# Another written order for the attention steps of a hybrid mixer

## The chip, the cores and the metric

The kernel runs on one core of a Trainium2 chip. The metric is device time in microseconds (us) of one execution. The core's engines work beside one another, each through its own queue in order: PE (TensorE, the matmuls), DVE (VectorE), ACT (ScalarE), POOL (GpSimd) and SP (SyncE, which issues the DMAs).

## The reference

Two layers, each on 256 tokens of width 1024 in float32. A layer adds half of a gated feed-forward (width 2816), then a mixer, then half of a second feed-forward:

```python
for l in range(DEPTH):
    x = x + 0.5 * swiglu_ffn(x, ffn1...)
    h = rms_norm(x, mix_norm[l])
    (fq, fk, fv, ff, gu, gv, nq, nkc, nvc, nks, nvs, nkw, nvw, ng, pz) = split(h @ w_in[l])
    o_a = fox_mixer(fq, fk, fv, ff)         # 4 heads, softmax attention with a forget bias
    o_b = gmlp_mixer(gu, gv)                # 4 gated groups
    o_c = nsa_mixer(nq, nkc, ..., ng)       # 4 heads: compressed + selected + window attention
    o_d = pool_mixer(pz)                    # 4 groups of running means
    x = x + concat([o_a, o_b, o_c, o_d]) @ w_out[l]
    x = x + 0.5 * swiglu_ffn(x, ffn2...)
```

With 256 tokens the selected and the window branch of nsa_mixer both are plain causal softmax attention over all tokens, over one key head of width 64 that four query heads share; the compressed branch has 15 keys that come out of a small two-layer network over windows of 32 tokens.

## The kernel before, in words

Everything is kept transposed, 128 features on the partitions and 256 tokens along the row. Weights and activations of the large products are split in two parts of reduced precision: a part h (ACT copies the raw weights, L122) and the remainder lo (DVE subtracts h from them, L123); a product is two or three matmuls (mm2, L147; mm3, L141). A weight block of 128 x 2048 thus costs a DMA into one of four raw buffers, two copies on ACT and two subtractions on DVE, the first halves ahead of the second. Where split() is called (by the first step of a generator such as out_part or z_proj), those four instructions stand in the ACT and DVE queues at that place.

The mixer first makes the projections. From the place named `here` on, its order is written out by hand as a list of calls, and pin() (L102) adds an edge from each PE, DVE and ACT instruction to the next of the same engine, so each of the three queues keeps exactly the order of the list. DMA issues (SP), POOL's instructions, and instructions outside the list, such as the next feed-forward's first weight copies, are placed between by the framework's scheduler.

In the list there are six attention jobs, each a pair of heads: F0 and F1 (fox) and N0 to N3 (nsa: two pairs, and for each the selected and the window branch). A job has these steps:

- scores(jb), L765: four matmuls into two PSUM banks; then on DVE four reductions that add the mask and take the row maxima (L779), and on ACT four exponentials with their sums (L781).
- scale(jb), L784: DVE's reciprocal of the sums (L787), a gate (L789) and four multiplications of the probabilities (L792).
- trans(jb), L794: six PE transposes into two banks (L799) and two copies out by ACT (L801).
- values(jb), L804: eight matmuls (L811) that need those copies.
- done(jb), L814: for an nsa pair one more matmul with the compressed branch's weights (L817); then the result is split into h (ACT, L134) and remainder (DVE, L135).

Between these stand filler blocks of PE work that need nothing from the attention: zq (a projection), cmp_hidden (the first layer of the compression network), pool_mix and pool_out (whose split is L137 on ACT and L138 on DVE), and steps of the output product, out_part (L829). The latter has four generators: w00 and w01 for the first half of the output columns, w10 and w11 for the second, the last digit for the half of the inputs. The first `go` of one calls split(); each of the 16 following steps is one mm3. The compressed branch goes through cmp_gelu (three pieces, parted by yields), cmp_out (two pieces; the first has DVE's vbd copies, L502), cmp_keys, cmp_scores (three pieces: mask; maximum and exponential, L738 to L740; sums and weights, L743 to L748) and cmp_weights (PE transposes, L755), which needs the last piece of cmp_scores and is needed by done(N1) and done(N3).

PSUM has eight banks, all drawn from one pool; a bank is taken at the first write and given back behind the last reader.

Of the kernel before, what the change touches and what calls it, by code (L numbers as in the profile page):

```python
# [70 lines left out]
def tile_macaron(ctx, tc, xT, g0, const0, consts, params, w13, w2, wA, wB, wD, wC, wE, wcmp, wo, out):  # L71
# [15 lines left out]
    def bank_a():  # L87
        a = banks.tile([128, 512], F32, name="a", tag="bank")
        return a

    def bank_h():
        h = banks.tile([128, 512], F32, name="h", tag="bank")
        return h
# [5 lines left out]
    def halves(s):  # L99
        return s.rearrange("p (a n) -> p a n", a=2)  # L100
# [248 lines left out]
    def mixer(l, norm, par):  # L349
        def Pm(name, p=128):  # L350
            o, w = _PAR[name]
            return par[0:p, o:o + w]
# [49 lines left out]
        def head_norm(ps, ht, nh, width):  # L402
            nt = [s2(), s2()]
            for t in range(2):
                nc.vector.tensor_tensor(nt[t][:, :width].rearrange("p (h d) -> p h d", d=64),
                                        ps[t][:, :width].rearrange("p (h d) -> p h d", d=64),
                                        ht[:, t, :nh].unsqueeze(2).to_broadcast([128, nh, 64]), op=ALU.mult)
            return nt
# [113 lines left out]
        def cmp_keys():  # L522
            p = bank_h()
            nc.tensor.transpose(p[:, 0:NC], e.kcn[0:NC, :], ident[0:NC, 0:NC])
            for par2 in range(2):
                rows = slice(64 * par2, 64 * par2 + 64)
                nc.vector.tensor_copy(kcz[rows, par2, 0:NC], p[rows, 0:NC])
# [81 lines left out]
        def pool_out():  # L609
            pw = Pm("pw").rearrange("p (c e) -> p c e", c=2)  # L610
            py = halves(bank_h())
            for c in range(2):
                nc.tensor.matmul(py[:, c, :], pw[:, c, :], e.po[:, c, :], start=True, stop=True)
            for c in range(2):
                oT[6 + c] = split_scaled(py[:, c, :], Pm("pscale")[:, c:c + 1])
# [9 lines left out]
        def b_post():  # L625
            nt = head_norm(e.pB, e.hB, 6, 384)
            nqk = w1p.tile([128, 2, 448], F32)
            nq = nqk[:, :, 0:384].rearrange("p t (h d) -> p t h d", d=64)
            for t in range(2):
                nc.vector.tensor_tensor(nqk[:, t, 0:384], nt[t][:, 0:384], Pm("ngain"), op=ALU.mult)  # L630
            ra = w1p.tile([128, 2, 6, 16], F32)
            rc = w1p.tile([128, 2, 6, 16], F32)

            def tab(i, c0, c1):
                return rope[:, i, :, c0:c1].unsqueeze(2).to_broadcast([128, 2, 6, c1 - c0])

            nc.vector.tensor_tensor(ra, nq[:, :, :, 0:16], tab(0, 0, 16), op=ALU.mult)
            nc.vector.tensor_tensor(rc[:, :, :, 0:8], nq[:, :, :, 8:16], tab(1, 0, 8), op=ALU.mult)
            nc.vector.tensor_tensor(rc[:, :, :, 8:16], nq[:, :, :, 0:8], tab(1, 8, 16), op=ALU.mult)
            nc.vector.tensor_tensor(nq[:, :, :, 0:16], ra, rc, op=ALU.add)  # L640
            nc.vector.tensor_copy(nqk[:, :, 384:448], nqk[:, :, 256:320])
            e.nqk = nqk

        def b_heads():
            nqT, nkT = halves(s2()), halves(s2())
            p = transposed([e.nqk[:, t, 128 * i:128 * i + 128] for i in range(2) for t in range(2)])
            nc.scalar.activation(nqT, p, AF.Copy)

            p = transposed([e.nqk[:, t, 256 + 64 * i:384 + 64 * i] for i in range(2) for t in range(2)])
            nc.scalar.activation(nkT, p, AF.Copy)  # L650
            e.nqT, e.nkT = nqT, nkT
# [111 lines left out]
        tcols = (slice(0, 128), slice(128, 384))  # L763

        def scores(jb):  # L765

            q, ks = jb.qk()
            s = [bank_h(), bank_h()]
            for t, c in enumerate(tcols):
                for i, rows in enumerate(half_rows):  # L770
                    nc.tensor.matmul(s[i][:, c], q[rows, 128 * t:128 * t + 128], ks[i][rows, 0:128 * t + 128],
                                     start=True, stop=True)
            bias = e.bias[jb.pair] if jb.branch is None else [(mask[:, 128:256], mask)] * 2
            jb.s = [s2(), s2()]
            jb.sm = at.tile([128, 2, 2], F32, name="sm")
            nm = at.tile([128, 2, 2], F32, name="nm")
            for i in range(2):
                for t, c in enumerate(tcols):
                    nc.vector.tensor_tensor_reduce(out=jb.s[i][:, c], in0=s[i][:, c], in1=bias[i][t], op0=ALU.add,  # L779
                                                   op1=ALU.min, scale=-1.0, scalar=3e38, accum_out=nm[:, t, i:i + 1])  # L780
                    nc.scalar.activation(jb.s[i][:, c], jb.s[i][:, c], AF.Exp, scale=-1.0, bias=nm[:, t, i:i + 1],  # L781
                                         accum_out=jb.sm[:, t, i:i + 1])

        def scale(jb):  # L784

            rv = at.tile([128, 2, 2], F32, name="rv")
            nc.vector.reciprocal(rv, jb.sm)  # L787
            if jb.branch is not None:
                nc.vector.tensor_tensor(rv, rv, e.g4[:, :, 2 * jb.pair:2 * jb.pair + 2, jb.branch], op=ALU.mult)  # L789
            for i in range(2):  # L790
                for t, c in enumerate(tcols):
                    nc.vector.tensor_scalar(jb.s[i][:, c], jb.s[i][:, c], rv[:, t, i:i + 1], None, op0=ALU.mult)  # L792

        def trans(jb):  # L794
            jb.pT = []
            for i in range(2):
                p = bank_h()
                for n in range(3):
                    nc.tensor.transpose(p[:, 128 * n:128 * n + 128], jb.s[i][:, 128 * n:128 * n + 128], ident)  # L799
                pT = s2()  # L800
                nc.scalar.activation(pT[:, 0:384], p[:, 0:384], AF.Copy)  # L801
                jb.pT.append(pT)

        def values(jb):  # L804

            if jb.branch != 2:
                e.acc[jb.pair] = bank_a()
            acc = e.acc[jb.pair]
            for tj, c, o in ((0, slice(0, 256), 0), (1, slice(256, 384), 128)):
                for i, rows in enumerate(half_rows):  # L810
                    nc.tensor.matmul(acc[rows, o:256], e.v[tj][:, jb.v[i]:jb.v[i] + 64], jb.pT[i][:, c],  # L811
                                     start=jb.branch != 2 and tj == 0, stop=jb.branch is None and tj == 1)

        def done(jb):  # L814
            acc = e.acc[jb.pair]
            if jb.branch is not None:
                nc.tensor.matmul(acc[:, 0:256], vbd[:, jb.pair, :], e.pcT, start=False, stop=True)  # L817
            oT[jb.pair + (0 if jb.branch is None else 4)] = split_scaled(acc[:, 0:256], None)
# [21 lines left out]
        N0, N1, N2, N3, F0, F1 = jobs  # L840
# [13 lines left out]
        def go(gen, n=1):  # L854
            for _ in range(n):
                next(gen, None)
# [15 lines left out]
        w00, w01 = out_part(0, 0, wacc), out_part(0, 1, wacc)  # L872
# [2 lines left out]
        cmp_hidden(0, 1)  # L875
        b_stats()
        scores(F0)
        go(zq)
        fox_bias(1)
        cmp_hidden(1, 0)  # L880
        scale(F0)
        b_post()
        scores(F1)
        go(zq)
        trans(F0)
        b_heads()
        cmp_hidden(1, 1)
        pool_mix()
        scale(F1)
        values(F0)  # L890
        scores(N0)
        gelu = cmp_gelu()
        go(gelu)
        trans(F1)
        go(w00, 4)
        done(F0)
        go(gelu)
        scale(N0)
        pool_out()
        values(F1)  # L900
        scores(N1)
        go(w01)
        done(F1)
        go(w00, 4)
        go(gelu)
        trans(N0)
        scale(N1)
        go(w00, 4)
        values(N0)
        scores(N2)  # L910
        go(w00, 5)
        outs = cmp_out()
        go(outs)
        trans(N1)
        wacc1 = [halves(bank_a()), halves(bank_a())]
        w10, w11 = out_part(1, 0, wacc1), out_part(1, 1, wacc1)
        go(w10)
        go(w01, 4)
        go(outs)
        values(N1)  # L920
        scale(N2)
        scores(N3)
        go(w01, 4)
        trans(N2)
        cmp_keys()
        go(w10, 3)
        cs = cmp_scores()
        go(cs)
        scale(N3)
        go(w11)  # L930
        go(w10, 1)
        values(N2)
        go(cs)
        go(w10, 4)
        trans(N3)
        go(w10, 5)
        go(cs)
        values(N3)
        go(w10, 4)
        cmp_weights()  # L940
        go(w11, 4)
        done(N1)
# [135 lines left out]
```

## Time and profile before

| | before |
|---|---|
| median of 3 runs | 983.79 us (981.37 to 986.28) |
| the profiled execution, its own time | 982.34 us |
| its span, first to last instruction | 980.5 us |
| mean granted TensorE clock | 0.996 |
| busy: PE / weight loads / DVE / ACT | 98% / 85% / 71% / 54% |
| instructions | 14915 |

The span is what the timeline covers; the execution's own time has some 1.8 us around it. Busy time of PE is that of its matmuls, which overlap one another: a matmul's duration is longer than the step to the next, so the pace of a block is read as the difference between the start of a block and the start of the next. [...] The first mixer's written list runs from about 232 to 300 us, the second's from about 715 to 784 us; times below are of the first unless said otherwise.

### The profile page before, as it was taken

How to read it: one execution, taken by the hardware profiler on the slowest of the kernel's cores; microseconds unless marked ns; L12 is line 12 of the kernel's file. 1: busy time of each engine (PE TensorE's matmuls, PEld its weight loads, DVE VectorE, ACT ScalarE, POOL GpSimd, SP SyncE). 2: the span in 40 equal slices, each digit the busy share in tenths (PEclk: the TensorE clock that was granted, in tenths of full speed). 3: DMA queues.
4: the chain of work that ended last, by engine and by line, in shares of the span. 5: the costliest groups of instructions: out<-in, count | busy, mean ns of one | idle time of the engine just before them, and what ended most of it. 6: DMA issues, size and time to landing. Idle time of an engine off the chain costs nothing. (4 is left out here: it accounts for less than half of the span.)

```text
span 980.5 us, 14915 instructions
## 1 busy us (share of the span) xinstructions
PE 964.3 (98%) x5840; PEld 838.0 (85%) x5840; DVE 698.6 (71%) x1256; ACT 530.6 (54%) x971; POOL 66.0 (7%) x67
## 2 busy tenths in 40 slices
PE   8999999999989999999999999999998999999998
PEld 6888888898869888888888888889987898888887
DVE  5987776575778777776667777755666787777751
ACT  7655555363566555655445655544545665555530
POOL 2000000031102000000010000001220030000000
PEclk9999999999999999999999999999999999999999
DMA  8965554445426655555555555545453455555530
GB/s 306 338 230 196 172 191 174 159 145 215 173 94 233 232 173 189 197 172 196 191 172 187 200 172 188 197 152 184 169 203 114 150 211 175 177 196 188 177 108 17
DMA packets 28150, 179.28 MB, mean 183 GB/s; under 512 B 3248, under 2 KB 5168, under 8 KB 8240
## 3 DMA queue, kind: packets, MB, share of 16 engines
q1 hardware_dynamic: 27792, 178.19, 52.1%
q8 instruction: 46, 0.75, 0.3%
q10 hardware_dynamic: 288, 0.14, 0.1%
q14 instruction: 24, 0.20, 0.1%
HBM read 177.27 MB, written 1.05 MB: 182 GB/s over the span
## 5 line engine op out<-in xcount | busy, mean ns | idle before, releaser
L123 DVE TENSOR_TENSOR lo<-r,h 128x1024 fp32r<-128x1024 f32 (+4 forms) x346 | 391.7, 1148 | 163.4 <-ACT h L122 162.7
L149 PE MATMUL h<-hl,h 128*128 128x512 f32 x1408 | 498.7, 399 | 1.4 <-ACT h L122 0.8
L122 ACT ACTIVATE h<-r 128x1024 fp32r<-128x1024 f32 (+4 forms) x346 | 327.8, 973 | 268.1 <-issue 230.6
L150 PE MATMUL h<-hl,lo 128*128 128x256 f32 x1408 | 395.3, 281 | 0.5 <-DVE lo L123 0.5
L149 PEld LDWEIGHTS h<-hl,h 128*128 128x128 f32 x1408 | 264.4, 188 | 67.9 <-DVE hl L138 1.5
L150 PEld LDWEIGHTS h<-hl,lo 128*128 128x128 f32 x1408 | 265.8, 189 | 2.1 <-DVE lo L123 2.1
L149 PE MATMUL a<-hl,h 128*128 128x512 f32 x704 | 246.9, 395 | 0.0
L150 PE MATMUL a<-hl,lo 128*128 128x256 f32 x704 | 197.3, 280 | 0.0
L149 PEld LDWEIGHTS a<-hl,h 128*128 128x128 f32 x704 | 131.9, 187 | 31.5 <-DVE hl L135 0.9
L150 PEld LDWEIGHTS a<-hl,lo 128*128 128x128 f32 x704 | 133.0, 189 | 0.0
L234 DVE SCALAR_TENSOR_TENSOR x<-a,x 128x256 f32<-128x256 f32 x80 | 32.9, 421 | 49.0 <-PE a L150 45.3
L304 DVE TENSOR_TENSOR s<-h,s 128x256 f32<-128x256 f32 x176 | 65.9, 415 | 1.1 <-ACT s L303 1.1
L305 DVE TENSOR_TENSOR s<-s,rb 128x512 f32<-128x512 f32 x88 | 60.9, 692 | 2.8
L134 ACT ACTIVATE hl<-s 128x256 fp32r<-128x256 f32 x92 | 38.2, 417 | 43.4 <-DVE s L308 33.9
L303 ACT ACTIVATE s<-h 128x256 f32<-128x256 f32 x176 | 56.5, 371 | 2.7 <-PE h L150 2.7
L211 POOL TENSOR_TENSOR s<-s 128x512 f32<-128x512 f32 x12 | 16.8, 1402 | 593.3 <-ACT s L207 593.3
L143 PE MATMUL a<-h,hl 128*128 128x384 f32 (+2 forms) x128 | 45.8, 358 | 0.0
L307 ACT ACTIVATE s<-s 128x256 f32<-128x256 f32 x88 | 35.5, 404 | 17.9 <-DVE s L305 17.8
L145 PE MATMUL a<-h,hl 128*128 128x384 f32 (+2 forms) x128 | 45.0, 351 | 0.0
L144 PE MATMUL a<-lo,hl 128*128 128x384 f32 (+2 forms) x128 | 44.9, 351 | 0.0
L135 DVE TENSOR_TENSOR hl<-s,hl 128x256 fp32r<-128x256 f32 x92 | 38.4, 419 | 3.4 <-ACT hl L134 3.4
L308 DVE TENSOR_TENSOR s<-s 128x256 f32<-128x256 f32 x88 | 36.8, 419 | 3.4 <-ACT s L307 3.4
(187 smaller groups left out, 779.1 us busy)
## 6 DMA issues: line engine op xcount, KB each, us to landing
r<-in_w_dram SPq DMA_DIRECT2D x129, 1024.0 KB, 4.8
r<-in_wcmp_dram SPq DMA_DIRECT2D x8, 1024.0 KB, 4.8
r<-in_wo_dram SPq DMA_DIRECT2D x8, 1024.0 KB, 5.4
r<-in_wE_dram SPq DMA_DIRECT2D x4, 1024.0 KB, 4.7
r<-in_wC_dram SPq DMA_DIRECT2D x4, 1024.0 KB, 4.7
r<-in_wD_dram SPq DMA_DIRECT2D x4, 800.0 KB, 4.3
r<-in_wA_dram SPq DMA_DIRECT2D x4, 768.0 KB, 4.4
r<-in_wB_dram SPq DMA_DIRECT2D x4, 768.0 KB, 4.3
```

The costliest lines, as they stand in the source:

```text
L122: nc.scalar.activation(h[:, c], r[:, c], AF.Copy)
L123: nc.vector.tensor_tensor(lo[:, c], r[:, c], h[:, c].bitcast(F32), op=ALU.subtract)
L134: nc.scalar.activation(th, src, AF.Copy)
L135: nc.vector.tensor_tensor(tl, src, th.bitcast(F32), op=ALU.subtract)
L143: nc.tensor.matmul(o, wgt[0], mov[0], start=start, stop=False)
L144: nc.tensor.matmul(o, wgt[0], mov[1], start=False, stop=False)
L145: return nc.tensor.matmul(o, wgt[1], mov[0], start=False, stop=stop)
L149: nc.tensor.matmul(o, wgt[0], mov[2], start=start, stop=False)
L150: return nc.tensor.matmul(o[:, :T], wgt[1], mov[0], start=False, stop=stop)
L303: nc.scalar.activation(hr[:, j, :], st[m][j][:, T:], AF.Copy)
L304: nc.vector.tensor_tensor(hr[:, j, :], st[m][j][:, :T], hr[:, j, :], op=ALU.add)
L305: nc.vector.tensor_tensor(hr, hr, st["rb"].unsqueeze(1).to_broadcast([128, 2, T]), op=ALU.mult)
```

## The change

The matmuls of a step's scores and its softmax become two functions, scores(jb) and softmax(jb), so that other PE work can be listed between them, and the list is written anew. Among what moves: trans(F0) goes ahead of the second z block; each scale is followed by the next job's scores, the transposes and then that job's softmax; the first piece of cmp_out goes behind the w10 weights; the third piece of cmp_gelu goes behind softmax(N1); the w01 weights are split behind done(F1) and ahead of scale(N1); pool_out goes ahead of scale(N0); and the w11 weights are split behind trans(N3), ahead of the last piece of cmp_scores. The number of w00, w01, w10 and w11 steps in the list is the same, in other portions. No instruction of the listed blocks is added or dropped.

```diff
--- before.py
+++ after.py
@@ -763,13 +763,16 @@
         tcols = (slice(0, 128), slice(128, 384))
 
         def scores(jb):
-
             q, ks = jb.qk()
-            s = [bank_h(), bank_h()]
+            jb.p = s = [bank_h(), bank_h()]
             for t, c in enumerate(tcols):
                 for i, rows in enumerate(half_rows):
                     nc.tensor.matmul(s[i][:, c], q[rows, 128 * t:128 * t + 128], ks[i][rows, 0:128 * t + 128],
                                      start=True, stop=True)
+
+        def softmax(jb):
+
+            s = jb.p
             bias = e.bias[jb.pair] if jb.branch is None else [(mask[:, 128:256], mask)] * 2
             jb.s = [s2(), s2()]
             jb.sm = at.tile([128, 2, 2], F32, name="sm")
@@ -875,68 +878,74 @@
         cmp_hidden(0, 1)
         b_stats()
         scores(F0)
+        softmax(F0)
         go(zq)
         fox_bias(1)
         cmp_hidden(1, 0)
         scale(F0)
+        scores(F1)
+        trans(F0)
+        softmax(F1)
         b_post()
-        scores(F1)
         go(zq)
-        trans(F0)
-        b_heads()
+        values(F0)
         cmp_hidden(1, 1)
         pool_mix()
         scale(F1)
-        values(F0)
-        scores(N0)
+        b_heads()
         gelu = cmp_gelu()
         go(gelu)
         trans(F1)
+        done(F0)
+        scores(N0)
+        softmax(N0)
+        go(gelu)
         go(w00, 4)
-        done(F0)
+        values(F1)
+        pool_out()
+        go(w00, 4)
+        scale(N0)
+        scores(N1)
+        trans(N0)
+        softmax(N1)
+        done(F1)
         go(gelu)
-        scale(N0)
-        pool_out()
-        values(F1)
-        scores(N1)
         go(w01)
-        done(F1)
-        go(w00, 4)
-        go(gelu)
-        trans(N0)
-        scale(N1)
         go(w00, 4)
         values(N0)
+        go(w00, 5)
+        scale(N1)
         scores(N2)
-        go(w00, 5)
-        outs = cmp_out()
-        go(outs)
         trans(N1)
+        softmax(N2)
         wacc1 = [halves(bank_a()), halves(bank_a())]
         w10, w11 = out_part(1, 0, wacc1), out_part(1, 1, wacc1)
         go(w10)
         go(w01, 4)
+        outs = cmp_out()
         go(outs)
         values(N1)
+        go(w01, 4)
         scale(N2)
         scores(N3)
-        go(w01, 4)
         trans(N2)
+        softmax(N3)
+        go(outs)
+        go(w10, 4)
+        values(N2)
         cmp_keys()
-        go(w10, 3)
+        go(w10, 2)
         cs = cmp_scores()
         go(cs)
+        go(w10, 4)
         scale(N3)
+        go(cs)
+        trans(N3)
         go(w11)
-        go(w10, 1)
-        values(N2)
-        go(cs)
-        go(w10, 4)
-        trans(N3)
         go(w10, 5)
         go(cs)
         values(N3)
-        go(w10, 4)
+        go(w10, 2)
         cmp_weights()
         go(w11, 4)
         done(N1)
```

## Rows read from the trace of the kernel before

**Rows 1.** The page: busy time, share of the span, instructions.
```profile
PE 964.3 (98%) x5840; PEld 838.0 (85%) x5840; DVE 698.6 (71%) x1256; ACT 530.6 (54%) x971; POOL 66.0 (7%) x67
```

**Rows 2.** Waits of PE, 228 to 302 us: total us, times, longest.
```profile
PE a L811 <- ACT s L801: 3.0, 2, 2.6
...
PE h L603 <- ACT s L593: 0.3, 1, 0.3
```

**Rows 3.** One window: length, busy shares (instructions), PEclk, DMA share, GB/s.
```profile
273.00:274.00 1.00, 1.00 (x8) 0.71 (x6) 0.96 (x4) 0.00 (x0) 0.00 (x0) 0.50 0.00 0
```

**Rows 4.** PE timeline: start, us, instruction, idle before and its releaser.
```profile
264.42 0.87 PE L811 MATMUL a<-s 128*64 128x256 f32 x8
...
265.22 0.93 PE L771 MATMUL h<-s 64*128 64x128 f32 x8
...
266.08 0.39 PE L143 MATMUL a<-hl,h 128*128 128x256 f32 x1
...
267.61 0.82 PE L799 MATMUL h<-c0t,s 128*128 128x128 f32 x6
...
272.50 1.92 PE L811 MATMUL a<-s 128*64 128x256 f32 x8 [2.65 <-ACT s L801]
...
277.45 0.55 PE L498 MATMUL h<-par,chv 128*128 128x64 f32 x4
...
278.26 0.88 PE L799 MATMUL h<-c0t,s 128*128 128x128 f32 x6
...
284.88 1.07 PE L799 MATMUL h<-c0t,s 128*128 128x128 f32 x6 [1.04 <-DVE s L792]
...
285.88 0.23 PE L524 MATMUL h<-c0t,kcn 15*128 15x15 f32 x1
...
290.98 0.82 PE L799 MATMUL h<-c0t,s 128*128 128x128 f32 x6
...
296.28 0.38 PE L755 MATMUL h<-c0t,pcm 128*128 128x128 f32 x2
...
756.32 1.50 PE L811 MATMUL a<-s 128*64 128x256 f32 x8 [2.64 <-ACT s L801]
```

**Rows 5.** ACT timeline, same columns.
```profile
265.26 0.46 ACT L137 ACTIVATE hl<-h,par 128x256 fp32r<-128x256 f32 x1
...
269.82 1.99 ACT L122 ACTIVATE h<-r 128x1024 fp32r<-128x1024 f32 x2
...
276.37 0.40 ACT L781 ACTIVATE s<-s,nm 128x128 f32<-128x128 f32 x1 [3.54 <-DVE nm L779]
...
278.05 0.19 ACT L781 ACTIVATION_READ_ACCUMULATOR s<-s,nm 128x1 f32 x1
...
278.85 0.88 ACT L801 ACTIVATE s<-h 128x384 f32<-128x384 f32 x2 [0.17 <-PE h L799]
```

**Rows 6.** DVE timeline, same columns.
```profile
267.33 0.48 DVE L138 SCALAR_TENSOR_TENSOR hl<-h,par,hl 128x256 fp32r<-128x256 f32 x1 [0.54 <-ACT hl L137]
...
273.17 0.42 DVE L135 TENSOR_TENSOR hl<-a,hl 128x256 fp32r<-128x256 f32 x1
...
274.65 0.17 DVE L787 RECIPROCAL rv<-sm 128x4 f32<-128x4 f32 x1
...
275.06 1.01 DVE L792 TENSOR_SCALAR s<-s,rv 128x128 f32<-128x128 f32 x4
...
278.05 0.92 DVE L502 COPY vbd<-h 32x64 f32<-32x64 f32 x4 [0.81 <-PE h L498]
...
289.84 2.35 DVE L123 TENSOR_TENSOR lo<-r,h 128x1024 fp32r<-128x1024 f32 x2
...
293.69 0.27 DVE L743 TENSOR_REDUCE csm<-sc 128x8 f32<-128x120 f32 x1
...
294.59 0.64 DVE L123 TENSOR_TENSOR lo<-r,h 128x512 fp32r<-128x512 f32 x1
...
295.54 0.28 DVE L748 TENSOR_TENSOR pcm<-sc,crv 128x120 f32<-128x120 f32 x1
```

## Prediction

> **What bounds the kernel now.** The page comes first: the matmul engine PE is busy for 98% of the span [rows 1], so 16 us of it are idle, and the rest of the program issues matmuls at a fixed pace that this change does not touch. What can move is PE's waiting inside the two mixers. The second view is PE's list of waits over the first mixer [rows 2]: 3.0 us for the copies of the transposed weights out of PSUM (L801) and 0.3 us for L593. [...] The fourth is PE's timeline [rows 4]. Values(N0) at 272.50 waited 2.65 us; then values, scores(N2) and four w00 steps took 277.45 - 272.50 = 4.95 us, while the same blocks take 0.80 + 0.86 + 1.53 = 3.19 us (264.42, 265.22, 266.08, 267.61). So the wait cost 2.65 us and then 1.76 us, most of it clock. Trans(N2) at 284.88 waited another 1.04 us. The second mixer has the same wait (756.32: 2.64 us).
>
> Waits name ACT and DVE, so those two come last. The order that pin() writes down is a queue for PE, for ACT and for DVE: on each of them an instruction that waits holds all behind it. I follow the new order through the three queues, in the first mixer's times.
>
> **The change, part by part.** No compute instruction is added or taken away in the listed blocks; what moves is who stands behind whom. Durations, from before: exponentials of one step 1.8 to 1.9 us on ACT (276.37 to 278.24), a pair of PSUM copies L801 0.8, a weight copy 1.0 per half [rows 5]; on DVE a weight remainder (L123) 1.15 per half, scale 0.4 of reciprocal and gate (274.65 to 275.06) and then 1.0, done plus the third gelu piece 1.48 (273.17 to 274.65), cmp_out's four vbd copies 0.9 [rows 6]; on PE cmp_out is 278.26 - 277.45 = 0.81 [rows 4]. Transposes that wait for a scale start 0.4 after it starts and issue until 0.5 after it ends (284.88 to 285.88, against a scale whose pattern is that of 275.06).
>
> *Until scores(N1).* Nothing differs up to cmp_hidden(1,0). Trans(F0) now stands straight behind scores(F1), and scale(F0) is not ready: I cost that at 0.45 us (bounds 0 and the 1.04 of trans(N2) [rows 4]). The L593 wait of 0.33 [rows 2] goes, because values(F0) and cmp_hidden now lie between. Scores(N1) ended at 266.08; now one more block of four w00 steps precedes it: 266.08 + 1.53 + 0.45 - 0.33 = 267.7.
>
> *Trans(N0).* Scale(N0) now stands behind pool_out's split on DVE. Pool_out ends about 267.7 - 0.86 - 1.53 = 265.3; its two halves alternate ACT 0.46, DVE 0.48 [rows 5, 6], one after the other since they read one bank: 267.35. Scale(N0) until 268.75, trans(N0) until 269.2. PE waits about 0.9 us in all.
>
> *Trans(N1), in place of the old wait.* On ACT: the second copy out of trans(N0) until 269.7, exponentials N1 until 271.5, done(F1) until 271.85, the w01 copies until 272.8 and 273.8. On DVE: done and gelu until 273.45 (1.48 plus a short wait for done's first half), then both w01 remainders, 275.75, and only then scale(N1): 276.15, so that trans(N1) starts at 276.6 and issues until 277.6. PE meanwhile has 1.53 + 0.85 + 1.53 + 0.86 = 4.8 us of work behind 269.2, until 274.0. It waits 2.6 us: the old wait for ACT is gone, and one of the same size for DVE stands there. What is late next is the remainder of w01, queued ahead of scale(N1).
>
> *Trans(N2).* ACT: copy out of trans(N1) until 278.05, exponentials N2 until 279.85, w10 copies until 281.8. DVE: w10 remainders until 283.15, then the vbd copies, which used to stand ahead of them, 284.05, then scale(N2): trans(N2) starts at 284.9. Before it started at 284.88 [rows 4]. PE has 277.6 + 1.53 + 0.81 + 0.85 + 1.53 + 0.86 = 283.2 and waits 1.7 us. So all that was won or lost until here is absorbed in this wait: the chain exponentials N2, w10 copies, w10 remainders runs at the same time as before. A clock that falls at trans(N1) also ends in it.
>
> *The end.* From trans(N2) to trans(N3) PE had 290.98 - 285.88 = 5.1 us of work; it now has two w10 steps more, 5.85, and trans(N3) issues until about 292.2 (scale(N3) waits for the scores behind the cmp keys, which takes about as long). Then DVE has the second piece of the cmp softmax, 0.5, ACT its exponential, 0.3, the copies out of trans(N3), 0.8, and only now w11: copies until 294.4 and 295.35, remainders until 296.75. Before, the w11 split stood ahead of trans(N3) and ahead of this softmax. Now the third piece of the softmax stands on DVE behind w11's remainder: 1.1 us if nothing comes between, 297.85, and cmp_weights at 297.95. It was at 296.28 [rows 4]. PE has six w10 steps and values(N3), 3.2 us, until 295.4 and waits 2.55. That is **+1.7 us a mixer**, and nothing later absorbs it, since PE has no wait in the tail or in the feed-forward behind it.
>
> Two prices stand on top. The next feed-forward's first weights, which pin() leaves free, had their remainders (0.64 each, four of them) between the pieces of this softmax: the third piece took 293.69 to 295.82, 2.1 us in place of 1.1 [rows 6]. There it was covered; now that stretch is on the path. None is the lower bound, all four, 2.6, the upper; I take the two that the trace shows there, **1.2 us**. And behind a wait of 2.5 us or more the clock may fall: nothing below, 1.76 above [rows 4]; I take **1.5 us**, as a part of the 1.76 was a second wait for half a copy, and both waits of that size in the trace were followed by slow matmuls (values in 1.92 and 1.50 us, 0.87 at 264.42).
>
> [...]
>
> DMAs: the order of the weight loads stays, each starts when a raw buffer comes free behind a remainder, and w11's comes free 4.6 us later (289.84 + 2.35 = 292.2 [rows 6], to 296.75); the load that it holds up is needed steps into the feed-forward, tens of us on. POOL has one small chain (the norm of kcn); its reader on DVE now stands behind scale(N2) and the softmax of N3, which cover it. I cost both at nothing; if the feed-forward did wait, it would be for part of 4.6 us a mixer.
>
> The sum: 1.7 + 1.2 + 1.5 = 4.4 us a mixer, 8.8 for two. On the profiled execution, 982.34 us (its span of 980.5 and 1.8 around it), that is 991.1; on the median of the runs, 983.79, 992.6. I say **991.5**.
>
> **Rivals.** *Late end alone.* If the free remainders stay out of the softmax and the clock holds, 2 x 1.7 = 3.4 us remain: 986. For it: PE's wait is only as long as those that cost clock in the old order, not longer. Against: both of those did cost it.
>
> *The clock falls at every wait.* Then trans(N2) and the blocks behind it, which are bound by PE's work until trans(N3), lose up to 1.5 us more, and all four remainders may come in between (1.4 more): 2 x 7.3 = 14.6, 997. For it: 1.7 us of waiting at trans(N2), right behind a wait of 2.6. Against: the wait of 1.04 us at 284.88 was followed by matmuls at full pace.
>
> *Faster: the DVE chains are shorter than I make them.* The place is DVE between scale(N0) and scale(N1), 7.0 us by my working against 4.8 of PE work, and between scale(N3) and the softmax's end, 6.1 against 3.2. From the point where these fit PE's work, the old waits go and nothing replaces them: 0.33 + 2.65 + 1.76 + 1.04 = 5.8 us a mixer, 971; with half of that, 977. For it: PE's wait in the trace is for ACT, not for DVE, and the exponentials now begin earlier. Against: two remainders of 1.15 us ahead of scale(N1) cannot begin before the w01 copy, which stands behind the exponentials N1 and done(F1).
>
> **How the numbers follow.** Forecast 0.45, late end alone 0.20, clock at every wait 0.20, faster 0.15. Under 0.5% (4.9 us) a measurement cannot tell this kernel from no change. Late end alone falls within that, and a small part of the forecast, where only one mixer pays for clock: same 0.23. Slower takes the rest of the forecast and the clock rival, 0.62; faster 0.15. The forecast's own range is 986 to 997; to hold the time 8 times in 10 it reaches to half of the faster rival and somewhat over the clock rival: 979 to 1000.
>
> **What would show it.** PE's waits in each mixer: L811 for L801 gone, L799 for L792 at trans(N1) about 2.6 us and at trans(N2) about 1.7, and L755 (cmp_weights) for L748 2.5 us or more, with a granted clock of 0.5 behind it; the mixer's end 2 to 6 us later against its start. It is wrong if PE reaches cmp_weights without a wait, or if trans(N2) starts clearly earlier in its mixer than before, for then the chain through the w10 copies is not what sets it.

## The result, and the profile after

The changed kernel takes 993.93 us (median of 4 runs, 991.26 to 995.35) against 983.25 of the kernel before beside it: a ratio of 1.0103, 95% interval 1.0067 to 1.0138. It is slower, 2.4 us above the forecast of 991.5 and inside its own range of 986 to 997.

The table cuts each mixer at four PE events and gives the stretches between them in both profiled executions. The start is the mixer's forget_sums matmul (L684), where the order of the two kernels is still the same; "next" is the first matmul of the feed-forward behind the mixer.

| us | before, mixer 1 / 2 | after, mixer 1 / 2 | more |
|---|---|---|---|
| start to trans(N2) | 53.78 / 53.90 | 53.97 / 53.54 | +0.19 / -0.36 |
| trans(N2) to trans(N3) | 6.10 / 6.09 | 6.99 / 8.23 | +0.89 / +2.14 |
| trans(N3) to cmp_weights | 5.30 / 5.31 | 8.40 / 8.39 | +3.10 / +3.08 |
| cmp_weights to next | 9.70 / 9.69 | 11.07 / 11.81 | +1.37 / +2.12 |
| mixer | 74.88 / 74.99 | 80.43 / 81.97 | +5.55 / +6.98 |

The two mixers lose 12.5 us. The span grew by 10.7 only (980.5 to 991.2), because the first mixer began 1.8 us earlier in this profile; its start lies at 229.0 to 231.1 us in the profiles of this case, and the rewritten list stands behind it. So mixers are compared from their own start. The line numbers of the attention steps are not those of before: scores is L770 here, the exponentials L784, scale L790 to L795, trans L802 and its copies L804.

The page, busy time (against [rows 1]). PE's work is the same 5840 matmuls; its share fell by a point:
```profile
PE 966.0 (97%) x5840; PEld 840.9 (85%) x5840; DVE 699.0 (71%) x1256; ACT 532.3 (54%) x971; POOL 68.0 (7%) x67
```

PE's waits of the changed kernel, 228 to 302 us (against [rows 2]: total, times, longest). The waits for ACT's copies (L801) and for L593 are gone; both names that stand there now are DVE's:
```profile
PE h L755 <- DVE pcm L748: 4.5, 1, 4.5
PE h L802 <- DVE s L795: 3.8, 3, 2.4
```

PE's timeline (against [rows 4]), in the first mixer trans(N0), trans(N1), trans(N2), trans(N3) and cmp_weights; then the same of the second mixer without trans(N0) and trans(N3). Trans(N3) comes without a wait, cmp_weights 8.40 us behind it, after a wait of 4.45:
```profile
266.20 1.16 PE L802 MATMUL h<-c0t,s 128*128 128x128 f32 x6 [0.43 <-DVE s L795]
...
274.44 1.59 PE L802 MATMUL h<-c0t,s 128*128 128x128 f32 x6 [2.38 <-DVE s L795]
...
283.25 1.16 PE L802 MATMUL h<-c0t,s 128*128 128x128 f32 x6 [0.96 <-DVE s L795]
...
290.24 0.82 PE L802 MATMUL h<-c0t,s 128*128 128x128 f32 x6
...
298.64 0.66 PE L755 MATMUL h<-c0t,pcm 128*128 128x128 f32 x2 [4.45 <-DVE pcm L748]
...
763.69 1.16 PE L802 MATMUL h<-c0t,s 128*128 128x128 f32 x6 [2.38 <-DVE s L795]
...
772.07 1.41 PE L802 MATMUL h<-c0t,s 128*128 128x128 f32 x6 [1.79 <-DVE s L795]
...
788.69 0.66 PE L755 MATMUL h<-c0t,pcm 128*128 128x128 f32 x2 [4.43 <-DVE pcm L748]
```

Windows of it (against [rows 3]; PEclk, the granted clock as a share of full speed, is the third number from the end). PE reads as fully busy at 0.50 behind trans(N1) and cmp_weights in the first mixer and behind trans(N2) in the second, as it did before behind values(N0) [rows 3]:
```profile
276.00:277.00 1.00, 1.00 (x7) 1.00 (x6) 0.21 (x2) 0.93 (x4) 0.00 (x0) 0.50 0.99 418
...
299.00:300.00 1.00, 1.00 (x7) 1.00 (x6) 1.00 (x3) 0.38 (x1) 0.00 (x0) 0.50 1.25 369
...
774.00:775.00 1.00, 1.00 (x6) 1.00 (x6) 0.81 (x6) 1.00 (x6) 0.00 (x0) 0.50 0.55 229
```

ACT's timeline behind trans(N3) (against [rows 5]): the exponential of the compressed softmax, the copies out of trans(N3), and then ten weight copies in one block (merged in one row), w11's two first:
```profile
291.08 0.30 ACT L740 ACTIVATE sc<-sc 128x120 f32<-128x120 f32 x1 [4.40 <-DVE sc L739]
291.29 0.85 ACT L804 ACTIVATE s<-h 128x384 f32<-128x384 f32 x2
292.03 6.16 ACT L122 ACTIVATE h<-r 128x1024 fp32r<-128x1024 f32 x10
```

DVE's timeline (against [rows 6]). First the w01 remainders that hold up the scale of N1 (274.10), then w11's remainders, and the third piece of the softmax (L743 to L748) with a free remainder of 512 columns behind each of its first four instructions:
```profile
271.43 2.35 DVE L123 TENSOR_TENSOR lo<-r,h 128x1024 fp32r<-128x1024 f32 x2
...
274.10 1.01 DVE L795 TENSOR_SCALAR s<-s,rv 128x128 f32<-128x128 f32 x4
...
293.12 2.36 DVE L123 TENSOR_TENSOR lo<-r,h 128x1024 fp32r<-128x1024 f32 x2 [2.08 <-ACT h L122]
295.40 0.27 DVE L743 TENSOR_REDUCE csm<-sc 128x8 f32<-128x120 f32 x1
295.59 0.68 DVE L123 TENSOR_TENSOR lo<-r,h 128x512 fp32r<-128x512 f32 x1
...
296.30 0.64 DVE L123 TENSOR_TENSOR lo<-r,h 128x512 fp32r<-128x512 f32 x1
...
296.94 0.68 DVE L123 TENSOR_TENSOR lo<-r,h 128x512 fp32r<-128x512 f32 x1
...
297.61 0.68 DVE L123 TENSOR_TENSOR lo<-r,h 128x512 fp32r<-128x512 f32 x1
298.22 0.28 DVE L748 TENSOR_TENSOR pcm<-sc,crv 128x120 f32<-128x120 f32 x1
```

### The profile page after: what moved, and what is told of

The parts are those of the page before. It is cut to its first block, busy times and chain, and to the rows that moved or that the text cites. A ratio compares the mean times of both kernels' runs of the same rounds, so it can differ in the third digit from the quotient of the medians.

```text
span 991.2 us, 14902 instructions
## 1 busy us (share of the span) xinstructions
PE 966.0 (97%) x5840; PEld 840.9 (85%) x5840; DVE 699.0 (71%) x1256; ACT 532.3 (54%) x971; POOL 68.0 (7%) x67
## 4 chain that ended last, share of the span: by engine, by line
PE 92%; DVE 4%; ACT 2%; DMA 1%; issue 1%; SPq 0%; POOL 0%
PE h L149 32%; PE a L149 16%; PE h L150 16%; PE a L150 8%; PE a L143 4%; PE a L144 4%; PE a L145 4%; DVE lo L123 2%; PE h L802 1%; PE h L143 1%; PE h L459 1%; PE h L144 1%; PE h L145 1%; ACT h L122 1%; ACT s L784 1%; DMA r<-in_w_dram 1%
## 5 line engine op out<-in xcount | busy, mean ns | idle before, releaser
L211 POOL TENSOR_TENSOR s<-s 128x512 f32<-128x512 f32 x12 | 16.8, 1401 | 595.4 <-ACT s L207 595.4
L143 PE MATMUL a<-hl,h 128*128 128x256 f32 x128 | 41.2, 322 | 0.1
```

What stands on the lines that cost most here:

```text
L143: nc.tensor.matmul(o, wgt[0], mov[0], start=start, stop=False)
```

## The experiments

The theory on trial is that of the prediction (A): DVE's queue order ahead of cmp_weights makes the loss, w11's remainders first, the free pieces and the clock on top. The rival (B) is that the loss lies in the rest of the new list, above all in the new DVE wait at trans(N1).

**The softmax ahead of w11** (on the changed kernel):
```diff
         trans(N3)
-        go(w11)
-        go(w10, 5)
         go(cs)
+        go(w11)
+        go(w10, 5)
         values(N3)
```


> The changed kernel with one exchange: the third piece of the compressed softmax stands ahead of the w11 split. Theory A (the end: DVE's w11 remainders and the free remainders ahead of that piece hold cmp_weights, and the clock falls behind the wait): the wait at cmp_weights, 4.4 us a mixer, goes to under 0.3, with it the slow clock behind it; about 10 us less than the changed kernel, 983 to 985. Theory B (the wait for DVE at trans(N1), 2.4 us with slow matmuls behind it, is what made it slower; the end only shows it): the wait at cmp_weights goes, but at least half of the loss stays, 988 or more.


Measured: 982.43 us (10 runs), ratio to before 0.9989 (0.9972 to 1.0005). One exchanged pair of calls takes back the whole loss. DVE's timeline of it: the third piece ends at 292.45, w11's remainders come behind it:
```profile
292.17 0.28 DVE L748 TENSOR_TENSOR pcm<-sc,crv 128x120 f32<-128x120 f32 x1
292.92 4.17 DVE L123 TENSOR_TENSOR lo<-r,h 128x1024 fp32r<-128x1024 f32 x5 [0.47 <-ACT h L122]
```
PE reaches cmp_weights 64.55 and 64.74 us into its mixers without a wait, while trans(N1) still waits 2.38 us in both. PE's timeline of the first:
```profile
274.44 1.38 PE L802 MATMUL h<-c0t,s 128*128 128x128 f32 x6 [2.38 <-DVE s L795]
...
293.83 0.38 PE L755 MATMUL h<-c0t,pcm 128*128 128x128 f32 x2
```
So a list that has this wait, the one the rival named, is as fast as the kernel before: B falls. That does not make the wait free: the w01 move below, which takes it away, gains some 4 us. All else in the new list together changes the two mixers by 149.87 - 148.73 = 1.1 us, within noise.

The mixers are 162.40 - 148.73 = 13.7 us shorter than in the changed kernel, the median only 11.5. Some of it is lost again in the feed-forward behind each mixer: by the profile POOL's second sum of squares (L211) took 4.96 us there, 1.75 in the changed kernel, and PE waited 1.22 us for the end of POOL's chain (L217):
```profile
307.33 4.96 POOL L211 TENSOR_TENSOR s<-s 128x512 f32<-128x512 f32 x1 [2.16 <-ACT s L207]
...
316.24 0.61 PE L224 MATMUL h<-c0t,s 128*128 128x1 f32 x4 [1.22 <-POOL s L217]
```
The second mixer and the kernel with both moves show the same wait, the other kernels do not. Why POOL was slow there is open.

**The same fault put into the kernel before:**
```diff
         scale(N3)
-        go(w11)
         go(w10, 1)
 ...
         trans(N3)
+        go(w11)
         go(w10, 5)
         go(cs)
```


> The kernel before with one move: the w11 split goes from ahead of trans(N3) to behind it, still ahead of the third piece of the compressed softmax. Theory A: that alone makes cmp_weights wait, some 2 us for the remainders, 2 us for the free remainders of the feed-forward and 1.5 us of slow clock, less what PE had in hand: 4 to 5 us a mixer, 991 to 994. Theory B: the end has little to do with it, 983 to 986.


Measured: 991.86 us (6 runs), ratio 1.0067 (1.0045 to 1.0088); A. PE's waits in the first mixer name the same L755, 3.2 us, beside the old one for ACT:
```profile
PE h L755 <- DVE pcm L748: 3.2, 1, 3.2
PE a L811 <- ACT s L801: 2.7, 1, 2.7
PE h L799 <- DVE s L792: 1.8, 1, 1.8
```
PE's timeline of the first mixer, trans(N3) and cmp_weights:
```profile
292.25 1.27 PE L799 MATMUL h<-c0t,s 128*128 128x128 f32 x6
...
300.60 0.66 PE L755 MATMUL h<-c0t,pcm 128*128 128x128 f32 x2 [3.23 <-DVE pcm L748]
```
From trans(N3) to the next feed-forward the mixers take 19.33 and 19.50 us, against 15.00 in both before: 8.8 us for two, and the medians differ by 8.65. The profiled execution, 996.40 us, lost some 4 us a mixer more between trans(N2) and trans(N3), where the clock was slow (last section); the median does not need them. The fault is enough without the rest of the change, and the exchange above shows that the rest makes no loss without the fault.

**PE kept busy in the wait:** 30 matmuls whose result nobody reads, ahead of cmp_weights of the changed kernel. They add 3.75 us of PE work a mixer.
```diff
         go(w10, 2)
+        keep = bank_h()
+        for _ in range(30):
+            nc.tensor.matmul(keep[:, 0:256], oT[2][0][:, 0:128], oT[2][0], start=True, stop=True)
         cmp_weights()
```


> The changed kernel with 30 matmuls of 256 columns, whose result nobody reads, in PE's queue ahead of cmp_weights (about 3.6 us within the wait of 4.4). They take no place of other work. If the slow clock behind the wait costs what the traces show (1.4 us in the first mixer, 2.1 in the second), 3 to 3.5 us less than the changed kernel, 990 to 991, with a granted clock of 1.00 behind cmp_weights. If the slow stretch is paid for elsewhere (work behind it waits for DVE or ACT anyway), no difference, 993 to 994.


Measured: 988.78 us (5 runs), ratio 1.0056 (1.0036 to 1.0075): added work makes it faster. PE's timeline: cmp_weights comes as late as ever, 8.38 us behind trans(N3), but its wait is 0.83:
```profile
295.03 3.75 PE L951 MATMUL h<-hl 128*128 128x256 f32 x30
...
299.61 0.41 PE L755 MATMUL h<-c0t,pcm 128*128 128x128 f32 x2 [0.83 <-DVE pcm L748]
```
Its window behind that, full clock (1.00) where the changed kernel had 0.50:
```profile
300.00:301.00 1.00, 1.00 (x11) 1.00 (x10) 1.00 (x3) 0.39 (x1) 0.00 (x0) 1.00 1.09 311
```
From cmp_weights to the next feed-forward it takes 9.74 us in both mixers, against 11.07 and 11.81: the clock's price is 1.3 and 2.1 us, and it went with the idle time (0.83 and 0.86 us of waiting here, 4.45 and 4.43 there), not with the work behind it, which is the same. That is 3.4 of some 5 us between the medians. Where the rest comes from is open: in this execution the work between the two mixers took 406.5 us, as in that of the next experiment, and in five of the other profiles 408.8 to 408.9, without a wait of PE in any of these seven.

**The free weights behind the softmax:** the feed-forward's first splits may be issued only after the last instruction of the softmax (L748).
```diff
-            w13s[m] = split(w13[l, f, m], 2048, cuts=4 if m < 3 else 2, loads=2 if first and m == 2 else 1)
+            def load():
+                return split(w13[l, f, m], 2048, cuts=4 if m < 3 else 2, loads=2 if first and m == 2 else 1)
+            if f == 1 and m < 2:
+                with tc.issue_after(held[0].ins):
+                    w13s[m] = load()
+            else:
+                w13s[m] = load()
 ...
-            nc.vector.tensor_tensor(pcm[:, :, 0:NC], sc8,
+            held[0] = nc.vector.tensor_tensor(pcm[:, :, 0:NC], sc8,
```


> The changed kernel, with the feed-forward's first two weight blocks' remainders on DVE held behind the last instruction of the compressed softmax (an ordering edge, no wait). Theory A: the third piece takes 1.1 us in place of 3.1, so cmp_weights comes 2.0 us earlier in each mixer; the clock still falls behind the 2.4 us wait that is left: 989 to 990.5. If the free remainders only filled gaps between dependent instructions, no difference: 993 to 994. If the feed-forward then waits for its weights, 994 or more.


Measured: 989.82 us (6 runs), ratio 1.0052 (1.0031 to 1.0074). DVE's timeline of the third piece (L749 to L754 in this kernel), now 1.23 us from first to last in place of 3.1:
```profile
296.41 0.27 DVE L749 TENSOR_REDUCE csm<-sc 128x8 f32<-128x120 f32 x1
...
297.36 0.28 DVE L754 TENSOR_TENSOR pcm<-sc,crv 128x120 f32<-128x120 f32 x1
297.56 3.09 DVE L123 TENSOR_TENSOR lo<-r,h 128x512 fp32r<-128x512 f32 x5
```
Trans(N3) to cmp_weights takes 6.54 us in both mixers, against 8.40 and 8.39. So the four pieces cost 1.86 us a mixer. The wait that is left at cmp_weights is 2.58 and 2.59 us.

**The w01 split moved up** to where both its engines idle (on the changed kernel):
```diff
         scale(F1)
+        go(w01)
         b_heads()
 ...
         go(gelu)
-        go(w01)
         go(w00, 4)
```


> The changed kernel with one step moved: the w01 split stands behind scale(F1), where ACT and DVE had idle time, instead of between the third gelu piece and scale(N1). Theory A: the chain from scale(N0) to the weights of the compressed branch is one queue of ACT and DVE work without slack, so each of its links moves: trans(N1) starts about 2.2 us earlier in its mixer without its wait of 2.4 us, trans(N2) and cmp_weights 1.5 to 2.2 us earlier, and the wait at cmp_weights becomes 2.5 us; two mixers give 4 to 6 us, 988 to 990 us. Rival B: as in my prediction, whatever is won ahead of trans(N2) is absorbed there, because the w10 copies and remainders ahead of scale(N2) run at the same time; trans(N2) still starts 45 us into the mixer's list, and the time stays at 993 to 994 us.


Measured: 989.53 us (6 runs), ratio 1.0075 (1.0053 to 1.0098). The interval overlaps that of the changed kernel, so the trace must decide. PE's waits in the first mixer:
```profile
PE h L755 <- DVE pcm L748: 4.4, 1, 4.4
PE h L802 <- DVE s L795: 2.2, 2, 1.8
PE h L770 <- ACT s L650: 1.0, 1, 1.0
```
The wait at trans(N1) is gone; trans(N2) starts 52.35 and 52.38 us into the mixers (53.97 and 53.54), cmp_weights 67.74 and 67.77 (69.36 and 70.16). That is A, smaller than expected: 1.0 us went to a new wait (L770), because the w01 copies now stand on ACT ahead of the copy in b_heads (L650) that scores(N0) reads. That the wait at cmp_weights would shrink to 2.5 us was wrong: it stayed at 4.45, since the chain from trans(N3) to it is the same.

**Both moves together:**
```diff
         scale(F1)
+        go(w01)
 ...
-        go(w01)
         go(w00, 4)
 ...
         trans(N3)
+        go(cs)
         go(w11)
         go(w10, 5)
-        go(cs)
```


> The changed kernel with both moves: the third softmax piece of the compressed branch ahead of the w11 split, and the w01 split behind scale(F1). If the chain has no slack (A): no wait at cmp_weights and none at trans(N1), cmp_weights 2 us earlier than in the kernel with the softmax moved alone, 977 to 980 us. If the w10 remainders at trans(N2) absorb what the w01 split gives (B): the same 982 to 983 us as with the softmax moved alone.


Measured: 978.37 us (12 runs), ratio 0.9958 (0.9936 to 0.9980). A: no wait at trans(N1) or cmp_weights, which comes 63.17 and 64.65 us into the mixers, against 64.55 and 64.74 with the exchange alone. Of the 2 us expected, 1.4 came in the first mixer and 0.1 in the second. Trans(N2) waits 1.80 us in both mixers; PE's timeline:
```profile
282.54 1.16 PE L802 MATMUL h<-c0t,s 128*128 128x128 f32 x6 [1.80 <-DVE s L795]
...
764.80 1.16 PE L802 MATMUL h<-c0t,s 128*128 128x128 f32 x6 [1.80 <-DVE s L795]
```
Its windows behind the two: full clock behind the first, 0.59 behind the second, which reaches trans(N3) in 8.51 us in place of 7.00:
```profile
284.00:285.00 1.00, 1.00 (x9) 1.00 (x10) 0.94 (x8) 1.00 (x5) 0.00 (x0) 1.00 1.05 442
...
766.00:770.00 4.00, 3.91 (x21) 2.98 (x21) 1.55 (x12) 2.24 (x10) 0.00 (x0) 0.59 0.36 150
```

**A list without such a place.** out_part's split is made two steps, copies on ACT and remainders on DVE, and each stands where its engine has time. A remainder still stands between a softmax and its scale, but right behind the row maxima, where DVE would wait for the exponentials. Some other steps move with them: the third gelu piece, done(F1), scale(N3) and the second piece of the compressed softmax.
```diff
         def out_part(d, q, accs):
 
-            h, lo = split(wo[l, d, q], 2048)
+            h = spl.tile([128, 2048], F32R)
+            lo = spl.tile([128, 2048], F32R)
+            r = raws.tile([128, 2048], F32)
+            nc.sync.dma_start(r, wo[l, d, q])
+            for i in (0, 1024):
+                nc.scalar.activation(h[:, i:i + 1024], r[:, i:i + 1024], AF.Copy)
+            yield
+            for i in (0, 1024):
+                nc.vector.tensor_tensor(lo[:, i:i + 1024], r[:, i:i + 1024], h[:, i:i + 1024].bitcast(F32), op=ALU.subtract)
             yield
             for c, kk in [(c, kk) for k2 in (0, 2) for c in range(4) for kk in (k2, k2 + 1)]:
 ...
         wacc = [halves(bank_a()), halves(bank_a())]
         w00, w01 = out_part(0, 0, wacc), out_part(0, 1, wacc)
-        go(w00)
+        go(w00, 2)
         go(bq, 2)
         cmp_hidden(0, 1)
 ...
         pool_mix()
         scale(F1)
+        go(w01, 2)
         b_heads()
         gelu = cmp_gelu()
 ...
         go(w00, 4)
         values(F1)
+        go(gelu)
         pool_out()
+        wacc1 = [halves(bank_a()), halves(bank_a())]
+        w10, w11 = out_part(1, 0, wacc1), out_part(1, 1, wacc1)
+        go(w10)
         go(w00, 4)
         scale(N0)
 ...
         trans(N0)
         softmax(N1)
-        done(F1)
-        go(gelu)
-        go(w01)
+        go(w10)
         go(w00, 4)
         values(N0)
         go(w00, 5)
         scale(N1)
+        done(F1)
+        go(w11)
         scores(N2)
         trans(N1)
         softmax(N2)
-        wacc1 = [halves(bank_a()), halves(bank_a())]
-        w10, w11 = out_part(1, 0, wacc1), out_part(1, 1, wacc1)
-        go(w10)
+        go(w11)
         go(w01, 4)
         outs = cmp_out()
 ...
         values(N2)
         cmp_keys()
+        scale(N3)
         go(w10, 2)
         cs = cmp_scores()
         go(cs)
-        go(w10, 4)
-        scale(N3)
+        trans(N3)
         go(cs)
-        trans(N3)
-        go(w11)
         go(w10, 5)
         go(cs)
         values(N3)
-        go(w10, 2)
+        go(w10, 6)
         cmp_weights()
         go(w11, 4)
```


> A list of its own on the changed kernel's functions: the split of each out_part weight is two steps, copies on ACT and remainders on DVE, and each stands where its engine is idle: w01 behind scale(F1), w10 copies behind pool_out and remainders behind softmax(N1), w11 copies behind done(F1) and remainders behind softmax(N2), so that no copy or remainder stands between a softmax and the scale that PE waits for next. Theory (the waits are all queue order, none is a need of PE's work): almost no wait of PE is left in the list, 971 to 975 us. Rival (the exponentials and the scales alone already take as long as PE's blocks between two transposes): waits of 0.5 to 1 us stay at each of trans(N1) to trans(N3), the time stays at 978 to 983 us.


Measured: 974.05 us (6 runs), ratio 0.9915 (0.9897 to 0.9934): faster than both kernels, and as the theory had it. It shows what the list as a whole gains, not what each move does. W10's remainders (L842 here) end as scale(N1) can begin, since ACT's exponentials of N1 last until 271.22:
```profile
269.47 2.36 DVE L842 TENSOR_TENSOR lo<-r,h 128x1024 fp32r<-128x1024 f32 x2
271.74 0.17 DVE L790 RECIPROCAL rv<-sm 128x4 f32<-128x4 f32 x1
```
PE's waits in its first mixer are all that is left (the second shows the same three):
```profile
PE h L770 <- ACT s L650: 1.0, 1, 1.0
PE h L802 <- DVE s L795: 0.6, 1, 0.6
PE h L524 <- DVE kcn L519: 0.2, 1, 0.2
```
The granted clock stays at full speed through both mixers, which take 71.17 and 71.16 us.

## Why the prediction was right, and where its sizes were off

The mechanism was right; the sum was too small. The mixers lost 12.5 us where it said 8.8, and 1.8 of that difference does not show in the total, since the first mixer happened to start earlier in this profile. So it is in part luck that the time came within 2.4 us of the forecast. The sign "2 to 6 us later" held for the first mixer's end (5.55) and was passed in the second (6.98). Step by step:

- *Until trans(N1): right.* Trans(F0) had no wait at all (0.45 said, 0 the lower bound), trans(N0) 0.43 (0.9 said). Trans(N1) waited 2.38 us for the scale behind w01's remainders (2.6 said), and the wait for ACT went.
- *Trans(N2) absorbs what came before: right, with a limit that was not seen.* It starts 53.97 and 53.54 us into the mixers, against 53.78 and 53.90. But what it absorbs is PE's time only. What shortens DVE's own chain ahead of scale(N2) does move it, as the w01 move showed (1.2 to 1.6 us). And it absorbs a slow clock, nearly all of it, only when the clock falls ahead of it: behind trans(N2) itself nothing is absorbed.
- *The end: right in place, somewhat small.* Without the free pieces and the clock, the two mixers lost 12.5 - 3.7 - 3.5 - 1.2 = 4.1 us, where 3.4 was said; trans(N3) came 0.89 us later behind trans(N2), not the 0.75 of the two added steps. With the free remainders held back the wait at cmp_weights was 2.58 us, and 2.55 was said. The exchanged calls show the cause. The feed-forward behind paid nothing for w11's later load, as was said: between the mixers it took 408.82 us, against 408.94.
- *Free pieces: the mis-sized term.* All four remainders came in between, 1.86 us a mixer, 3.7 in all, not 1.2 a mixer, 2.4 in all. Before, two of them stood within the third piece (one is shown in [rows 6]) and two ahead of it; with w11 placed later their copies stood on ACT behind w11's and ended between 294.6 and 296.1 us, so none could run ahead of the piece (295.40), and all four came within it. The upper bound of 2.6 covered that, the chosen value did not. The first three of them before:
```profile
292.29 0.68 DVE L123 TENSOR_TENSOR lo<-r,h 128x512 fp32r<-128x512 f32 x1
...
293.08 0.68 DVE L123 TENSOR_TENSOR lo<-r,h 128x512 fp32r<-128x512 f32 x1
...
293.88 0.68 DVE L123 TENSOR_TENSOR lo<-r,h 128x512 fp32r<-128x512 f32 x1
```
- *Clock behind cmp_weights: right.* 1.37 and 2.12 us, 3.5 in all, where 3.0 was said.
- *Clock behind trans(N2): missed.* In the second mixer the 2.38 us wait at trans(N1) left the clock at 1.00, trans(N2) then waited 1.79, and the clock fell to 0.50 there: 8.23 - 6.99 = 1.2 us. That is a part of the second rival (the clock falls at every wait), in one mixer of two. The argument against it, the 1.04 us wait that cost nothing, was one of a shorter wait.

"Faster" failed because the DVE chains were as long as worked out: 6.8 us from the end of scale(N0) to scale(N1), where 7.0 was said, and 8.0 from the end of scale(N3) to that of the softmax, of which 1.9 are the free pieces, where 6.1 was said without them. Where the last list made them fit PE's blocks, 974.05 us came out, between the 971 and 977 that this rival was priced at.

That only one of two alike waits pays for the clock, a case to which the prediction gave a small part of its chance, no row of before shows: both waits there, 2.65 and 2.64 us, were followed by slow matmuls. The runs do show it: of the two 1.80 us waits of the kernel with both moves, which end 52.38 and 52.35 us into their mixers, the second was followed by slow matmuls (a clock of 0.59 over four microseconds), the first was not (1.00).

## What to carry to other kernels

In queues that run in order, ask of every weight copy and remainder which short chain stands right behind it, and whether PE waits for the end of that chain; here 2.4 us of work that nobody needed for a while, with what came on top of it, cost 4.5 and 5.2 us between trans(N3) and the end of the mixers, and exchanging two calls gave it back. Work that the list leaves free falls into the gaps of exactly such a chain, and is free only as long as the chain has slack. In this program a wait of PE of some 2 us has to be counted with what the clock may take behind it, 1.2 to 2.1 us in the changed kernel, and near the end of the mixer nothing gave that back.

## What the runs showed of the hardware that was not expected

The length of a wait did not decide alone what the clock did. The waits at cmp_weights, 2.58 to 4.45 us, were followed by slow matmuls (a granted clock of 0.50) in all eight mixers of the four kernels that have them (the changed one, its two forms with the free weights held back and with w01 moved up, and the kernel before with w11 late); the waits of 2.65 us at values(N0), in the kernel before and in that last one, in two of four. The wait of 2.38 us at trans(N1) occurs in eight mixers of four kernels (the changed one and the first, third and fourth above). Slow matmuls followed it in five; in the other three the clock was full (1.00) behind it, and in all three it fell behind the next wait instead, that of 1.8 us at trans(N2), where nothing absorbs it. In the five, trans(N2) found PE late, waited 1 us or less, and full clock (1.00) followed. Where the clock fell early, trans(N2) came at most 0.4 us later for it; where it fell late, the mixer lost 1.2 to 1.5 us.

In the kernel before with w11 late, the 2.65 us wait at values(N0) left the clock at 1.00, and the 1.76 us wait at trans(N2) was followed by 0.50 for ten microseconds, in both mixers alike, with PE busy throughout. Its windows:
```profile
283.00:288.00 5.00, 5.00 (x23) 4.52 (x21) 1.65 (x12) 2.56 (x10) 0.00 (x0) 0.50 0.31 126
288.00:293.00 5.00, 5.00 (x25) 4.25 (x25) 1.43 (x6) 0.30 (x1) 0.00 (x0) 0.50 0.00 0
```
The stretches at 0.50 elsewhere in the mixers lasted 3 to 4 us, and 6 to 7 in two mixers, where the clock fell 2 us or more before the wait at cmp_weights ended. What made those of ten microseconds so long stays open. They cost 4 us a mixer: trans(N2) to trans(N3) took 10.12 and 10.02 us, against 6.10 and 6.09. This profiled execution, 996.40 us, was the longest of its kernel's six (median 991.86), so most of them cannot have paid as much.
